# Layer 0, first strips: sums of squares and the shift's matrix product on four 32-column quarters of TensorE

## The chip, the cores and the metric

The kernel runs on one core of a Trainium2 chip. The metric is the time of one execution on the device, in microseconds (us). The engines that a core has are TensorE (PE; its weight loads are shown as PEld), VectorE (DVE), ScalarE (ACT), GpSimd (POOL) and SyncE (SP); SP, ACT and POOL also issue DMAs. Each engine works off its own instructions in the order in which they were written down, and waits on semaphores where another engine or a DMA has to come first.

## What is computed

A trunk of two layers on 1024 tokens of width 1024, all in float32. Layer 0 is a state-space mixer, layer 1 a forgetting attention. Only the head of layer 0 matters here:

```python
def _rms(x, g):
    xf = x.astype(jnp.float32)
    y = xf * lax.rsqrt(jnp.mean(xf * xf, axis=-1, keepdims=True) + EPS)
    return (y * g.astype(jnp.float32)).astype(x.dtype)

def _modulation(c, w, b, n):
    m = jax.nn.silu(c) @ w + b
    return jnp.split(m[:, None, :], n, axis=-1)
...
        if layer < N_A_LAYERS:
            shift, scale, gate = _modulation(c, a_mod_w[i], a_mod_b[i], 3)
            h = _rms(x, a_norm_g[i]) * (1.0 + scale) + shift
            y = _s5_mixer(h, a_w_in[i], ...)   # u, z = jnp.split(h @ w_in, 2, axis=-1)
```

So three vectors of 1024 come from silu(c) and a weight of 1024 x 3072; the first third of them is the shift.

## The kernel before, in words

x comes transposed: 8 strips of 128 features (partitions) by 1024 tokens, called xt. The normalisation is moved behind the projection. What is projected is x times the scale; the factor of each token, q2, is multiplied onto the result (`et`, line 323), and the shift's part, one number for each output row, is added as a bias. To get that number the activations have two more columns behind the 1024 tokens, columns 512 and 513 of the second half, that hold the shift (lines 300 to 303). Each float32 operand of a projection is split into a high and a low part (`aH`, `aL`, `w_hi`, `w_lo`), and three products of these are added up (`in_part`).

The modulation vectors are made by VectorE: `gemv` (line 132) multiplies a 128 x 1024 tile of the transposed weight with silu(c), spread over all partitions, and sums along the row. Tile n gives 128 entries of the vector.

The order of work, in the program's text:

1. A loop over 8 strips (line 272): load and gemv the tile of the scale (8 + k), load xt, make s_a, split the scaled strip into aH and aL, square it on ScalarE (`sqx`), and add up the squares over the partitions with two 128 x 512 float32 matmuls against a 128 x 128 matrix of 1/1024 (line 288). Each row of the result `msx` holds the same 1024 sums.
2. The projections `u01` for weight strips 0 and 1 over the 8 strips, tokens 0 to 767 (lines 290 to 292).
3. The load and split of weight strip 2, then 8 gemvs for the shift (lines 298 to 303), each followed by the two columns in aH (ScalarE) and aL (VectorE).
4. q2 from msx (`neg2_rsqrt`, line 153): six ScalarE and six VectorE operations on halves of 512.
5. Strip 2 in pieces of 512 and 256 tokens, then, for strips 0 to 3, the piece of 258 columns that holds the shift (c == 2 in `u_strip`), and strip 3's other pieces. For each strip `ut` (line 340, one buffer) is filled on ScalarE and written to memory (line 343).
6. The preparation of the state space: the angles `th`, `ang` (from line 373), sine and cosine (lines 387, 388), powers (`pwr`, `pwi`), and from the loads of B and C (`bb`, `bbs`, `x1m`, `x2m`, lines 469 to 473) the matrices `wm` and `moa`, which the matmuls `pin` and `pk` (lines 557, 569) read first. `pk` is a group of four matmuls that write 32 partitions each, on column quarters 0, 32, 64, 96 of TensorE.

The program's text is not the order in which the engines work: a scheduler writes down the order of each engine, by its own estimate of when things are ready, and `tc.issue_after` holds instructions behind a given one. All loads go through SP in the written order. The tiles of weights and x share seven buffers (tag `xw`), the projections' results two PSUM buffers (tag `pj`), so a copy out of PSUM must end before the second next piece starts.

Of the kernel before, what the change touches and what calls it, by code (L numbers as in the profile page):

```python
# [12 lines left out]
F32 = mybir.dt.float32  # L13
F32R = mybir.dt.float32r
BF16 = mybir.dt.bfloat16
AF = mybir.ActivationFunctionType
# [4 lines left out]
P = 128  # L21
D = 1024
KT = D // P
L = 1024
NG = 64
# [6 lines left out]
HL = L // 2  # L32
# [14 lines left out]
def trunk(tc, a, out):  # L47
    nc = tc.nc
    V, S, G, T, Q = nc.vector, nc.scalar, nc.gpsimd, nc.tensor, nc.sync
    top = ExitStack()  # L50
    with top:
# [4 lines left out]
        pj = top.enter_context(tc.tile_pool(name="pj", bufs=2, space=PSUM))  # L56
# [3 lines left out]
        def ctile(shape, nm, dt=F32):  # L60
            return cst.tile(shape, dt, name=nm, tag=nm)
# [4 lines left out]
        onesm = ctile([P, P], "onesm")  # L66
# [2 lines left out]
        G.memset(eps_t, EPS)  # L69
        one_t = ctile([P, 1], "one_t")  # L70
        G.memset(one_t, 1.0)
        vecs = ctile([P, 98], "vecs")
        c_b = modp.tile([P, D], F32, name="c_b", tag="c_b", bufs=1)
        Q.dma_start(out=c_b, in_=a["c"].broadcast_to([P, D]))
        Q.dma_start(out=vecs, in_=a["vecs"])
        vec, at0 = {}, 0
        for nm, w in (("a_g", 8), ("kv_g", 8), ("b_g", 8), ("b_glu", 8), ("kg", 1), ("qg", 1), ("modb", 64)):
            vec[nm] = vecs[:, at0:at0 + w]
            at0 += w
        fb_t = ctile([NH, 1], "fb_t")  # L80
# [48 lines left out]
        mod = ctile([P, 64], "mod")  # L129
# [5 lines left out]
        def modulate(n0, n1):  # L135
            for n in range(n0, n1):
                mw = mwp.tile([P, D], F32, name="modw", tag="modw")
                Q.dma_start(out=mw, in_=a["modw"][n])
                gemv(mw, n)

        def mod_bias(lo, hi, nm):
# [40 lines left out]
        with l0:  # L182
            s5 = l0.enter_context(tc.tile_pool(name="s5", bufs=1, reuse_waits="tile"))
# [66 lines left out]

            def mod_tile(n):
                mw = xp.tile([P, D], F32, name="mwx", tag="xw", bufs=7)
                d = Q.dma_start(out=mw, in_=a["modw"][n])
                gemv(mw, n)
                return d

            CH = ((0, 0, 512), (1, 0, 256), (1, 256, 514))
            TOK = (0, 512, 768)
# [9 lines left out]
            wu = pj.tile([P, HL], F32, name="wu", tag="pj")  # L268
            for _ in range(18):
                T.matmul(wu[:, 0:P], onesm, onesm, start=True, stop=True)  # L270
            mps = [pj.tile([P, HL], F32, name=f"msx{i}", tag="pj") for i in range(2)]
            for k in range(KT):
                mod_tile(8 + k)
                xt = xp.tile([P, L], F32, name="xt", tag="xw", bufs=7)
                Q.dma_start(out=xt, in_=a["xT"][:, k, :])
                if k < 2:
                    w01[k] = weight_strip(a["a_w_in"][k], [P, KT, P])
                V.scalar_tensor_tensor(out=s_a[:, k:k + 1], in0=mod[:, 8 + k:9 + k], scalar=sc1[:, k:k + 1], in1=ga[:, k:k + 1],
                                       op0=ALU.add, op1=ALU.mult)
                for i in range(2):  # L280
                    hi, xs = act[0][k][i][:, 0:HL], xt[:, HL * i:HL * i + HL]
                    S.activation(hi, xs, AF.Copy, scale=s_a[:, k:k + 1])
                    V.scalar_tensor_tensor(out=act[1][k][i][:, 0:HL], in0=xs, scalar=s_a[:, k:k + 1], in1=hi.bitcast(F32),
                                           op0=ALU.mult, op1=ALU.subtract)
                sq = xp.tile([P, L], F32, name="sqx", tag="sqx", bufs=2)
                sq_end = S.activation(sq, xt, AF.Square).ins
                for i in range(2):
                    T.matmul(mps[i], onesm, sq[:, HL * i:HL * i + HL], start=(k == 0), stop=(k == KT - 1))
            for k in range(KT):
                for e in range(2):  # L290
                    for c in range(2):
# [2 lines left out]
            Q.dma_start(out=raw2, in_=a["a_w_in"][2])  # L294
            w2 = [xp.tile([P, KT, P], F32R, name=f"w2{i}", tag=f"w2{i}") for i in range(2)]
            split(raw2, *w2)
            for k in range(KT):
                last_mod = mod_tile(k)
                hi, b = act[0][k][1][:, HL:], vec["modb"][:, k:k + 1]
                m = mod[:, k:k + 1].broadcast_to([P, 2])  # L300
                S.activation(hi, m, AF.Identity, bias=b)
                last_lo = V.scalar_tensor_tensor(out=act[1][k][1][:, HL:], in0=m, scalar=b, in1=hi.bitcast(F32),
                                                 op0=ALU.add, op1=ALU.subtract).ins
# [863 lines left out]
def pack(inp):  # L1167
    f = {k: np.asarray(v) for k, v in inp.items()}

    def strips(w, n=P):  # L1170
        m = w.shape[1]
        return w.reshape(KT, P, m // n, n).transpose(2, 1, 0, 3)

    def cols(v):
        return v.reshape(-1, P).T


    perm = np.arange(D).reshape(KT, 8, GC).transpose(0, 2, 1).reshape(-1)
# [6 lines left out]
    d = dict(  # L1185
        xT=f["x"][0].T.reshape(KT, P, L).transpose(1, 0, 2),
        c=f["c"].reshape(1, D),
        modw=modw.reshape(64, P, D),
        vecs=np.concatenate([cols(f["a_norm_g"][0]), cols(f["kv_norm_g"]), cols(f["b_norm_g"][0]), cols(f["a_b_glu"][0]),
                             np.concatenate([f["k_norm_g"]] * 2).reshape(P, 1),  # L1190
                             np.concatenate([f["q_norm_g"][0]] * 2).reshape(P, 1), cols(modb)], 1),
        f_bias=f["kv_f_bias"].reshape(NH, 1),
        A_re=f["a_A_re"][0].T, A_im=f["a_A_im"][0].T, log_dt=f["a_log_dt"][0].reshape(NG, 1),
        B_re=f["a_B_re"][0].transpose(1, 0, 2), B_im=f["a_B_im"][0].transpose(1, 0, 2),
        C_re=f["a_C_re"][0].transpose(2, 0, 1), C_im=f["a_C_im"][0].transpose(2, 0, 1),
        D=np.pad(f["a_D"].reshape(KT, 2, 4, GC).transpose(2, 3, 0, 1), ((0, 0), (0, 32 - GC), (0, 0), (0, 0))).reshape(P, 2 * KT),
        a_w_in=strips(f["a_w_in"][0]), a_w_glu=strips(f["a_w_glu"][0]), a_w_out=strips(f["a_w_out"][0]),
        kvq_w=np.concatenate([strips(f["kv_w"][:, D:2 * D], 256), strips(f["kv_w"][:, 0:D], 256),
                              strips(f["b_w_in"][0][:, 0:D], 256)], 0),
        kv_wf=strips(f["kv_w"][:, 2 * D:], NH)[0],  # L1200
        b_wz=strips(f["b_w_in"][0][:, D:]), b_w_out=strips(f["b_w_out"][0]),
    )
    return {k: np.ascontiguousarray(v) for k, v in d.items()}
# [13 lines left out]
```

## Time and profile before

| what | value |
|---|---|
| median of 3 runs | 1225.78 us (1220.67 to 1227.47) |
| the profiled execution | 1223.69 us |
| its span (first to last instruction) | 1221.9 us |
| mean granted TensorE clock | 0.987 of full speed |
| busy: TensorE, VectorE, ScalarE, GpSimd | 95%, 69%, 50%, 30% |
| busy from 0 to 160 us: TensorE, VectorE, ScalarE | 147.0, 136.7, 100.9 us |

Times in the profile count from the start of the span. In a list of instructions the columns are start, duration, engine, line, operation, output and inputs, shape and count, and in brackets the idle time of the engine ahead of it with what ended it. Rows that merge several instructions have a count, as x4. A float32 matmul shows as two records.

### The profile page before, as it was taken

To read this page: it belongs to the slowest core of one execution; us is meant where nothing else is said; L and a number is where in the kernel's file an instruction comes from. 1 tells how busy PE (TensorE), PEld (TensorE's weight loads), DVE (VectorE), ACT (ScalarE), POOL (GpSimd) and SP (SyncE) were. 2 spreads that over 40 slices of the span, in tenths; PEclk is the share of its full clock that TensorE was granted. 3 is DMA by queue.
4 is the path that set the end of the run, shared out by engine and by line. 5 is a ranking of instruction groups with operands and counts; after the bars stand their busy time and mean duration, and the time that the engine had idled before them with its cause. 6 is when DMAs were issued, how large, how long until landed. Compare 5 with 4: busy or idle time off the path is not lost.

```text
span 1221.9 us, 20599 instructions
## 1 busy us (share of the span) xinstructions
PE 1162.0 (95%) x7542; PEld 1017.3 (83%) x7542; DVE 848.9 (69%) x1724; ACT 605.1 (50%) x1138; POOL 367.8 (30%) x568
## 2 busy tenths in 40 slices
PE   8989898997899998899989999999999999999898
PEld 6778887887778876799989989998888888888686
DVE  7889899874498767746444664448787778887421
ACT  6565766665335324322213452227677777886310
POOL 4000000000000033600133463447576666764100
PEclk9999999998989999999999999999999999999999
DMA  9754666584974885247543277518796968871242
GB/s 352 220 173 117 171 169 164 154 233 126 334 249 129 281 312 167 90 154 233 200 148 139 83 214 152 156 70 182 132 188 124 171 122 155 156 138 27 94 165 78
DMA packets 113333, 205.30 MB, mean 168 GB/s; under 512 B 17072, under 2 KB 58160, under 8 KB 111696
## 3 DMA queue, kind: packets, MB, share of 16 engines
q1 hardware_dynamic: 86272, 161.44, 41.4%
q0 software_dynamic: 24960, 37.75, 18.1%
q10 hardware_dynamic: 2000, 4.79, 1.7%
q8 instruction: 60, 0.98, 0.3%
q14 instruction: 41, 0.34, 0.1%
HBM read 146.47 MB, written 46.20 MB: 158 GB/s over the span
## 4 chain that ended last, share of the span: by engine, by line
PE 57%; DVE 16%; DMA 12%; ACT 5%; issue 5%; SPq 2%; POOL 2%; ACTq 0%; POOLq 0%; DVEq 0%
PE tkps L851 16%; PE zb L112 7%; PE pj_f L112 5%; PE tp L1043 5%; DMA modw<-modw 4%; PE u L264 4%; PE ov L1049 3%; PE ov L1050 3%; PE sp L1010 3%; DMA v_d<-vt 3%; PE sp L1011 3%; PE pj_g L112 2%; DMA mwx<-modw 2%; PE f L112 2%; DVE w_lo L101 1%
## 5 line engine op out<-in xcount | busy, mean ns | idle before, releaser
L851 PE MATMUL tkps<-wvh,aH 128*128 128x256 f32 (+1 forms) x768 | 220.5, 287 | 7.3 <-DVE vt L863 4.0
L851 PE MATMUL tkps<-wvh,aL 128*128 128x256 f32 (+1 forms) x768 | 217.1, 283 | 1.4 <-DVE aL L167 1.4
L851 PE MATMUL tkps<-wvl,aH 128*128 128x256 f32 (+1 forms) x768 | 216.7, 282 | 0.0
L851 PEld LDWEIGHTS tkps<-wvh,aH 128*128 128x128 f32 x768 | 145.2, 189 | 9.8 <-DVE vt L863 4.9
L851 PEld LDWEIGHTS tkps<-wvh,aL 128*128 128x128 f32 x768 | 145.1, 189 | 2.1 <-DVE aL L167 1.8
L851 PEld LDWEIGHTS tkps<-wvl,aH 128*128 128x128 f32 x768 | 145.3, 189 | 0.3 <-issue 0.2
L1045 ACT ACTIVATE pth<-tp 128x512 fp32r<-128x512 f32 (+1 forms) x192 | 87.2, 489 | 61.4 <-PE ov L1049 34.7
L1018 ACT ACTIVATE pr<-pr,mx 128x128 f32<-128x128 f32 (+7 forms) x128 | 98.9, 773 | 22.4 <-DVE mx L1015 21.8
L1020 POOL TENSOR_SCALAR pr<-pr,sm 128x128 f32<-128x128 f32 (+7 forms) x128 | 96.2, 761 | 40.6 <-DVE sm L1019 40.5
L1046 DVE TENSOR_TENSOR ptl<-tp,pth 128x512 fp32r<-128x512 f32 (+1 forms) x192 | 101.3, 551 | 9.0 <-ACT pth L1045 8.6
L93 ACT ACTIVATE w_hi<-w_raw 128x1024 fp32r<-128x1024 f32 x49 | 51.6, 1053 | 86.4 <-PE pj_f L112 29.5
L1015 DVE CUSTOM_DVE_ANT_0 pr<-sp,fb 128x512 f32<-128x512 f32 (+3 forms) x128 | 72.8, 569 | 21.3 <-PE tp L1043 19.9
L1049 PE MATMUL ov<-pth,vhl 128*128 128x256 f32 x320 | 85.6, 299 | 0.1
L1043 PE MATMUL tp<-ident,pr 128*128 128x128 f32 x576 | 82.9, 273 | 0.0
L874 ACT ACTIVATE hsq<-tkps 128x256 f32<-128x256 f32 x64 | 24.6, 384 | 117.8 <-PE tkps L851 112.5
L132 DVE CUSTOM_DVE_ANT_0 modw<-modw,c_b 128x1024 f32<-128x1024 f32 x48 | 58.6, 1223 | 34.0 <-DMA modw<-modw 33.7
L1050 PE MATMUL ov<-ptl,vhl 128*128 128x256 f32 x320 | 81.0, 286 | 0.2 <-DVE ptl L1046 0.2
L1010 PE MATMUL sp<-kk,qs 128*128 128x256 f32 (+2 forms) x192 | 74.5, 388 | 2.2 <-DVE mx L1015 1.9
L1043 PEld LDWEIGHTS tp<-ident,pr 128*128 128x128 f32 x576 | 65.3, 140 | 7.1 <-POOL pr L1020 0.5
L794 POOL TENSOR_TENSOR sq<-sq,sq 128x512 f32<-128x512 f32 x12 | 19.0, 1585 | 173.3 <-ACT sq L790 173.3
L877 POOL TENSOR_TENSOR hms<-hms,nhalf 128x4 f32<-128x4 f32 x64 | 67.6, 1057 | 5.0
L876 POOL TENSOR_SCALAR hms<-hms 128x4 f32<-128x4 f32 x64 | 15.2, 237 | 176.3 <-DVE hms L875 172.4
(325 smaller groups left out, 3305.4 us busy)
## 6 DMA issues: line engine op xcount, KB each, us to landing
modw<-modw SPq DMA_DIRECT2D x48, 512.0 KB, 5.1
kk<-k_d POOLq DMA_DIRECT2D x32, 512.0 KB, 6.8
wvr<-kvq_w SPq DMA_DIRECT2D x12, 1024.0 KB, 5.5
mwx<-modw SPq DMA_DIRECT2D x16, 512.0 KB, 7.5
w_raw<-a_w_in SPq DMA_DIRECT2D x16, 512.0 KB, 5.2
v_d<-vt SPq DMA_DIRECT2D x32, 256.0 KB, 2.5
fb<-f_d SPq DMA_DIRECT2D x16, 512.0 KB, 8.9
vhl<-v_d POOLq DMA_DIRECT2D x16, 512.0 KB, 9.7
```

The source lines that it names most:

```text
L112: T.matmul(ps, w[wt][:, k, :], act[at][k][half], start=(k == k0 and n == 0), stop=(k == k1 and n == 2))
L851: T.matmul(ps[:, 0:nv], at, wt[:, k, 0:nv], start=(n == 0), stop=(n == 3 * KT - 1))
L877: G.tensor_tensor(out=ms, in0=ms, in1=nhalf, op=ALU.pow)
L1010: T.matmul(sp[:, 0:wm_], qsl, kk[:, 0, lo:lo + wm_], start=True, stop=False)
L1015: V.tensor_tensor_reduce(out=pr[:, lo:hi], in0=sp[:, 0:w_], in1=fb[:, lo:hi], scale=1.0, scalar=3e38 if m0 is None else m0, op0=ALU.add, o ...
L1018: S.activation(pr[:, 0:nk], pr[:, 0:nk], AF.Exp, scale=-1.0, bias=mx, accum_out=sm)
L1020: G.tensor_scalar(out=pr[:, 0:nk], in0=pr[:, 0:nk], scalar1=sm, scalar2=0.0, op0=ALU.mult, op1=ALU.add)
L1043: T.transpose(out=tp[:, b, :], in_=prs[qi][:, P * (b0 + b):P * (b0 + b) + P], identity=ident)
L1045: S.activation(pth[:, 0:m, dst], tp[:, 0:m, :], AF.Copy)
L1046: V.tensor_tensor(out=ptl[:, 0:m, dst], in0=tp[:, 0:m, :], in1=pth[:, 0:m, dst].bitcast(F32), op=ALU.subtract)
L1049: T.matmul(ov, vhl[:, b, :], pth[:, b - b0, :], start=(b == 0), stop=False)
L1050: end = T.matmul(ov, vhl[:, b, :], ptl[:, b - b0, :], start=False, stop=(b == nb - 1)).ins
```

## The change

Four things change, all in the head of layer 0.

- The sums of squares: the four squares of strips 0 to 3, and then those of 4 to 7, go as one group of four matmuls onto the four column quarters of TensorE, each 128 rows by 32 columns and 512 tokens, into 32 partitions of PSUM each (`quarters`). So 16 full matmuls become 4 groups of four. The result `msx` then holds four partial sums, 32 times each; ScalarE copies it to `mq`, and a matmul with a matrix of 1/32 (`o32`) for each half adds the four up over the partitions (`msy`).
- The shift: its weights come untransposed (`mod_sh`, 8 strips of 128 inputs by 1024 outputs), and the product is made by TensorE, with silu(c) as weights, 32 equal columns for each strip (`cs`): 4 groups of four matmuls (`psh`). ScalarE copies them to `shr`; eight small matmuls with two columns of `o32` (`pm`) add up the quarters and put the vector across the partitions. aH and aL of the two shift columns are then made out of PSUM (`pm`) instead of out of `mod`. The 8 gemvs and their 8 tile loads in the old layout go.
- Buffers: of the 8 strips of mod_sh, 0 to 3 use the `xw` buffers, 4 to 7 the buffers of `ut`, `bbs`, `x1m` and `x2m`. `sqx` has four buffers instead of two.
- The scratch memory for descriptors of DMAs that POOL issues is set to 8192.

```diff
+            def quarters(ps, ws, xs, first, last):
+                m = T.matmul(ps[96:P, :], ws[3], xs[3], start=first, stop=last).ins
+                with tc.issue_after(m):
+                    for q in range(3):
+                        T.matmul(ps[32 * q:32 * q + 32, :], ws[q], xs[q], start=first, stop=last)
...
-                sq = xp.tile([P, L], F32, name="sqx", tag="sqx", bufs=2)
+                sq = xp.tile([P, L], F32, name="sqx", tag="sqx", bufs=4)
                 sq_end = S.activation(sq, xt, AF.Square).ins
-                for i in range(2):
-                    T.matmul(mps[i], onesm, sq[:, HL * i:HL * i + HL], start=(k == 0), stop=(k == KT - 1))
+                sqs.append(sq)
+                if k % 4 == 3:
+                    for i in range(2):
+                        quarters(mps[i], [onesm[:, 0:32]] * 4, [t[:, HL * i:HL * i + HL] for t in sqs[-4:]], k == 3, k == KT - 1)
+            mq = xp.tile([P, L], F32, name="mq", tag="sqx", bufs=4)
+            for i in range(2):
+                S.activation(mq[:, HL * i:HL * i + HL], mps[i], AF.Copy)
+            mps = [pj.tile([P, HL], F32, name=f"msy{i}", tag="pj") for i in range(2)]
+            for i in range(2):
+                T.matmul(mps[i], o32, mq[:, HL * i:HL * i + HL], start=True, stop=True)
...
+            mws = []
             for k in range(KT):
-                last_mod = mod_tile(k)
+                pool, tag = ((s5, "ut"), (s5, "bbs"), (s5, "x1m"), (s5, "x2m"))[k - 4] if k >= 4 else (xp, "xw")
+                mws.append(pool.tile([P, D], F32, name="mws", tag=tag, bufs=7 if pool is xp else 1))
+                with tc.issue_after(last_x):
+                    last_mod = Q.dma_start(out=mws[k], in_=a["mod_sh"][k])
+            psh = [pj.tile([P, HL], F32, name=f"psh{i}", tag="pj") for i in range(2)]
+            for r in range(2):
+                for i in range(2):
+                    quarters(psh[i], [cs[:, k] for k in range(4 * r, 4 * r + 4)],
+                             [t[:, HL * i:HL * i + HL] for t in mws[4 * r:4 * r + 4]], r == 0, r == 1)
+            shr = xp.tile([P, D], F32, name="shr", tag="sqx", bufs=4)
+            for i in range(2):
+                S.activation(shr[:, HL * i:HL * i + HL], psh[i], AF.Copy)
+            pm = pj0.tile([P, NG], F32, name="pm", tag="dps")
+            for k in range(KT):
+                T.matmul(pm[:, 2 * k:2 * k + 2], shr[:, P * k:P * k + P], o32[:, 0:2], start=True, stop=True)
+            for k in range(KT):
                 hi, b = act[0][k][1][:, HL:], vec["modb"][:, k:k + 1]
-                m = mod[:, k:k + 1].broadcast_to([P, 2])
+                m = pm[:, 2 * k:2 * k + 2]
                 S.activation(hi, m, AF.Identity, bias=b)
                 last_lo = V.scalar_tensor_tensor(...)
...
-    nc = bacc.Bacc("TRN2", target_bir_lowering=False, num_devices=1)
+    nc = bacc.Bacc("TRN2", target_bir_lowering=False, num_devices=1, dynamic_dma_scratch_size=8192)
```

The scheduler writes a new order. The loads on SP behind the last strip of x, before:

```order
L275 DMA xt<-xT 128x1024
L294 DMA w_raw<-a_w_in 128x1024
L253 DMA mwx<-modw 128x1024 x8
L470 DMA bb<-B_re 64x1024
L471 DMA bb<-B_im 64x1024
L470 DMA bbs<-B_im 64x1024
L85 DMA w_raw<-a_w_in 128x1024
L471 DMA bbs<-B_re 64x1024
L470 DMA x1m<-C_re 64x1024
L471 DMA x1m<-C_im 64x1024
```

And after (mws are the strips of mod_sh; the first four are strips 4 to 7):

```order
L288 DMA xt<-xT 128x1024
L324 DMA mws<-mod_sh 128x1024 x4
L508 DMA bb<-B_re 64x1024
L315 DMA w_raw<-a_w_in 128x1024
L509 DMA bb<-B_im 64x1024
L324 DMA mws<-mod_sh 128x1024
L527 DMA fb_t<-f_bias 16x1
L324 DMA mws<-mod_sh 128x1024
L528 DMA dsk<-D 128x16
L324 DMA mws<-mod_sh 128x1024 x2
L85 DMA w_raw<-a_w_in 128x1024
L508 DMA x2m<-C_im 64x1024
```

The loads of B into bb stand ahead of the last strips now; those into x2m, bbs and x1m follow them, in this order, and wait for the matmuls psh that read these buffers.

ScalarE from the columns of the shift (aH out of mod) to the sine (the activation behind the table load, line 387), before:

```order
L301 ACTIVATE aH_1_165<-mod,vecs 128x2
L472 ACTIVATE x1m<-x1m,sg_pm 128x1024
L375 ACTIVATE th<-th 128x64 x7
L473 ACTIVATE x2m<-x2m 128x1024
L93 ACTIVATE w_hi<-w_raw 128x1024
L392 ACTIVATE ang_759<-th 128x448
L340 ACTIVATE ut<-et,bi 128x32x8
L340 ACTIVATE ut<-et,bi 128x64x8
L396 ACTIVATE ylo<-ang_759 128x64
L399 ACTIVATE xhi<-ang_759 128x64
L340 ACTIVATE ut<-et,bi 128x32x8
L387 ACT_TABLE_LOAD
```

After, from the last of the eight aH (out of pm; ahead of the eight stand now shr, x2m and x1m) to the same table load, line 425:

```order
L339 ACTIVATE aH_1_165<-pm,vecs 128x2
L413 ACTIVATE th<-th 128x64 x7
L93 ACTIVATE w_hi<-w_raw 128x1024
L378 ACTIVATE ut<-et,bi 128x32x8
L378 ACTIVATE ut<-et,bi 128x64x8
L378 ACTIVATE ut<-et,bi 128x32x8
L430 ACTIVATE ang_792<-th 128x448
L378 ACTIVATE ut<-et,bi 128x32x8
L378 ACTIVATE ut<-et,bi 128x64x8
L378 ACTIVATE ut<-et,bi 128x32x8
L425 ACT_TABLE_LOAD
```

x1m and x2m have moved ahead of the eight aH, and the three pieces of ut for strip 1 ahead of the sine. Each aH now also waits for the aL of the strip before it, since both engines read pm.

ScalarE in the second block of the state space, before (cT and sT are the tables of cosine and sine, r the gelu, which needs another table):

```order
L523 ACTIVATE cT<-sT 128x1024
L93 ACTIVATE w_hi<-w_raw 128x1024
L340 ACTIVATE ut<-et,bi 128x32x8
L631 ACT_TABLE_LOAD
L631 ACTIVATE r_1380<-py 128x512
L524 ACT_TABLE_LOAD
L524 ACTIVATE cT<-cT,hpi 128x1024
L525 ACTIVATE sT<-sT,tpi 128x1024
L543 ACTIVATE moa<-x1m 128x4x16
L631 ACT_TABLE_LOAD
```

And after:

```order
L561 ACTIVATE cT<-sT 128x1024
L549 DMA v_1330<-v_1329 64x1024 x2
L562 ACTIVATE cT<-cT,hpi 128x1024
L563 ACTIVATE sT<-sT,tpi 128x1024
L93 ACTIVATE w_hi<-w_raw 128x1024
L378 ACTIVATE ut<-et,bi 128x32x8
L669 ACT_TABLE_LOAD
L669 ACTIVATE r_1413<-py 128x512
```

cos and sin stand ahead of the gelu, and two of the three table loads are gone. Behind this place the order of every engine is that of before.

More of the change, by code (lines that the diff above doesn't have):

```diff
@@ L71, in trunk @@
         G.memset(one_t, 1.0)
-        vecs = ctile([P, 98], "vecs")
+        vecs = ctile([P, 106], "vecs")
         c_b = modp.tile([P, D], F32, name="c_b", tag="c_b", bufs=1)
@@ L76, in trunk @@
         vec, at0 = {}, 0
-        for nm, w in (("a_g", 8), ("kv_g", 8), ("b_g", 8), ("b_glu", 8), ("kg", 1), ("qg", 1), ("modb", 64)):
+        for nm, w in (("a_g", 8), ("kv_g", 8), ("b_g", 8), ("b_glu", 8), ("kg", 1), ("qg", 1), ("modb", 64), ("c", 8)):
             vec[nm] = vecs[:, at0:at0 + w]
@@ L137, in modulate @@
                 mw = mwp.tile([P, D], F32, name="modw", tag="modw")
-                Q.dma_start(out=mw, in_=a["modw"][n])
+                Q.dma_start(out=mw, in_=a["modw"][n - KT])
                 gemv(mw, n)
@@ L252, in mod_tile @@
                 mw = xp.tile([P, D], F32, name="mwx", tag="xw", bufs=7)
-                d = Q.dma_start(out=mw, in_=a["modw"][n])
+                Q.dma_start(out=mw, in_=a["modw"][n - KT])
                 gemv(mw, n)
-                return d
             CH = ((0, 0, 512), (1, 0, 256), (1, 256, 514))
@@ L274, in trunk @@
                 xt = xp.tile([P, L], F32, name="xt", tag="xw", bufs=7)
-                Q.dma_start(out=xt, in_=a["xT"][:, k, :])
+                last_x = Q.dma_start(out=xt, in_=a["xT"][:, k, :]).ins
                 if k < 2:
```

9 lines of the change are left out of this document (7 added, 2 removed).

## Prediction

> **What bounds the kernel now.** I read the page first. TensorE is busy for 95% of the span, but the share is an average, and the change lies in the first 60 us. So I took the windows there (columns: PE, PEld, DVE, ACT and POOL busy, granted clock, DMA share, GB/s).
>
> ```profile
> 10.00:15.00 5.00, 4.33 (x9) 2.33 (x10) 4.25 (x11) 3.85 (x5) 4.67 (x1) 0.66 1.02 406
> 38.00:40.00 2.00, 2.00 (x8) 1.25 (x7) 2.00 (x5) 0.06 (x1) 0.00 (x0) 1.00 1.01 381
> 42.00:44.00 2.00, 2.00 (x13) 1.73 (x13) 2.00 (x6) 2.00 (x6) 0.00 (x0) 1.00 1.02 231
> 60.00:70.00 10.00, 6.72 (x49) 6.38 (x50) 9.03 (x30) 8.13 (x16) 0.00 (x0) 0.97 0.42 111
> 90.00:100.00 10.00, 10.00 (x83) 9.23 (x81) 9.74 (x17) 7.07 (x14) 0.00 (x0) 1.00 0.33 97
> ```
>
> Up to 40 us the DMA is full at about 400 GB/s; behind that it stays full at half the rate, because then the loads of B and C run, which fill 64 partitions each. From 70 to 120 us TensorE has no gap, and VectorE is close behind it. Between the two lies a stretch where TensorE waits. The chain of waits names what it waited for (start, us, what):
>
> ```profile
> 26.62 7.70 DMA mwx<-modw
> 35.59 7.76 DMA mwx<-modw
> 43.38 10.86 DMA x1m<-C_im
> 54.31 1.15 ACT x1m L472
> 59.65 0.34 DVE et L323
> 60.13 6.23 PE u L264 x48
> ...
> 69.49 18.63 PE u L264 x96
> 88.12 0.44 PE pin L557 x4
> ```
>
> The shift's weights hold up the last load of C (x1m); that holds up ScalarE, ScalarE the angles (th, ang) on VectorE, these the copy that frees a PSUM buffer, and that TensorE. The timeline of TensorE has the gaps, and the start of each strip:
>
> ```profile
> 25.32 0.68 PE L264 MATMUL u<-aL,w_hi 128*128 128x256 f32 x1
> 43.69 0.40 PE L264 MATMUL u<-aH,w 128*128 128x512 f32 x1
> 52.10 0.28 PE L264 MATMUL u<-aH,w_hi 128*128 128x258 f32 x1
> 60.13 0.36 PE L264 MATMUL u<-aH,w 128*128 128x258 f32 x1 [2.10 <-DVE et L323]
> 69.49 0.76 PE L264 MATMUL u<-aH,w_hi 128*128 128x512 f32 x1 [3.15 <-DVE bi L337]
> 70.06 0.63 PE L264 MATMUL u<-aL,w_hi 128*128 128x512 f32 x1
> ```
>
> At 43.69 strip 2 starts, at 52.10 the columns that hold the shift. The gaps of 2.10 and 3.15 us cost 5.3 us; after the second the matmuls run at half clock (0.63 us where 0.40 is usual), six or so of them, some 1.4 us more.
>
> **The sums of squares.** Before, 16 float32 matmuls of 128x512 make them.
>
> ```profile
> 20.95 1.88 PE L288 MATMUL msx<-sqx,onesm 128*128 128x512 f32 x4
> 21.38 0.19 PEld L288 LDWEIGHTS msx<-sqx,onesm 128*128 128x128 f32 x1 [0.24 <-issue]
> 21.81 0.19 PEld L288 LDWEIGHTS msx<-sqx,onesm 128*128 128x128 f32 x1 [0.24 <-issue]
> 88.49 0.32 PE L569 MATMUL pk<-moa,bb 128*32 128x128 f32 x4
> 88.49 0.43 PE L569 MATMUL pk<-moa,bb 128*32 128x128 f32 x8
> 88.85 0.30 PEld L571 LDWEIGHTS pk<-dd,ident 128*128 128x128 f32 x2 [0.20 <-issue]
> ```
>
> One matmul is two records, 0.43 us apart, so 0.86 us; 16 are 13.8. What four on quarters cost, the kernel shows already: pk is such a group, four matmuls in eight records. A look at 88.53 to 88.56 holds four of them (first pk row), so four had begun within 0.07 us of each other. A record of 128 columns follows the one before after a quarter of 0.43, 0.11 us: in a row the eighth would start 0.75 us after the first. Yet all eight have ended 0.43 us after it began, so the four run side by side. I cost a group at two records (0.86) plus 0.1 for the switch of tiling (the 0.20 idle of the loads behind pk): 0.95 us. The sums take 4 groups, 3.8 us, and 2 full matmuls (msy), 1.7: 5.5 instead of 13.8. The other bound is four in a row, 3.44 us a group.
>
> The Trainium skill, "TensorE: Matmul & The Clock Gate", section "Measured speedup vs the span model", gives 2.38 times for three column tiles; at that share of the ideal, a group would be an estimated 1.1 us, and the sum 1 us longer.
>
> TensorE then has, from 25.3 on, what it had until 43.69 without its last three pairs of sums (18.4 - 3 x 1.72 = 13.2 us), one pair of groups (1.9) and msy (1.7): it is free at 42.1. With fewer matmuls its clock may stay low for longer (0.66 in the window 10 to 15, after an idle stretch): 0 to 3.4 us; I take 1.5, so 43.6.
>
> **The shift.** Eight gemvs leave VectorE:
>
> ```profile
> L132 DVE CUSTOM_DVE_ANT_0 mwx<-mwx,c_b x16: 1159/1215/1225, 8.4 to 48.4; 128x1024 f32<-128x1024 f32 x16
> 49.63 0.30 ACT L301 ACTIVATE aH<-mod,vecs 128x2 fp32r<-128x2 f32 x1 [2.19 <-DVE mod L132]
> 50.98 0.21 DVE L302 SCALAR_TENSOR_TENSOR aL<-mod,vecs,aH 128x2 fp32r<-128x2 f32 x1
> 54.31 1.15 ACT L472 ACTIVATE x1m<-x1m,sg_pm 128x1024 f32<-128x1024 f32 x1 [4.38 <-DMA x1m<-C_im]
> 55.36 1.12 ACT L375 ACTIVATE th<-th 128x64 f32<-128x64 f32 x7
> ```
>
> 8 x 1.22 = 9.7 us, but most of that time VectorE then idles. The same 4 MB of weights must land. Before, the seventh strip landed at 43.35 (35.59 + 7.76); now six of the eight loads of B and C are behind all of them, so I take 43.3 (42 to 45). TensorE is ready then. psh: 4 groups, 3.8 us, to 47.4. Four pm matmuls (two loads each like the 0.30 of pk's last) 1.2, then strip 2's two pieces (52.10 - 43.69 = 8.4) with four pm between them (1.2): the columns of the shift are reached at 58.2, 6.1 later than before.
>
> The weights of strips 4 to 7 lie in the buffers of ut, bbs, x1m, x2m, so six loads now wait for psh: issued from 47.2, 1.57 MB. At the 231 GB/s of the window they need 6.8 us; with some 2 us to start they land at 56 (at 400 GB/s: 53). SyncE has further behind them only the writes of ut and the strips of weights, which aren't due before 60. On ScalarE the eight aH now stand behind x2m and x1m, so they start at 57.2 instead of 37 to 50, and each waits for the aL before it: 8 x (0.30 + 0.21) = 4.1, bounds 2.5 to 5. The angles are behind them: th ends at 62.5 instead of 56.5, 6 us late. Shift columns and angles are therefore both late by 6. What TensorE gains is that its two gaps shrink, since VectorE's copies for strips 0 and 1 are no longer behind the wait for th: its strip 3 starts at about 72 (when strip 1's ut, below, frees a buffer of et), against 69.49 and the 1.4 of slow clock, so 1 us behind.
>
> The sine is what is late next:
>
> ```profile
> 57.44 2.14 DVE L383 SCALAR_TENSOR_TENSOR th<-ang,th 128x512 f32<-128x512 f32 x3
> 60.16 1.77 ACT L340 ACTIVATE ut<-et,bi 128x256 f32<-128x256 f32 x2
> 64.04 0.26 ACT L387 ACTIVATE ang<-th 128x64 f32<-128x64 f32 x1
> u_d<-ut SPq DMA_DIRECT2D x8, 512.0 KB, 3.5
> 85.22 0.62 DVE L197 TENSOR_TENSOR wm<-wm,tm 128x448 f32<-128x448 f32 x1
> ```
>
> Before, it came at 64.04, ahead of strip 1's ut. Now it stands behind it, and ut has one buffer. The copies of strip 0 followed the end of th (56.5) by 3.2 us; two of the three steps of 0.7 between are now behind them, so they start 1.8 after 62.5, at 64.3. The ut of strip 0, three pieces of about 2.3 us in all (1.77 for two), ends at 67, its write lands 3.5 us later, ut of strip 1 takes 2.3 and the table 1.3 (rows below): the sine comes at 74.2, 10 us late. From the sine to wm VectorE needed 21.2 us (85.22 + 0.62 - 64.04 = 21.8, less the sine); the same work without its idle pieces is 19 to 20, so wm is ready at 94 instead of 85.8. TensorE reached pin at 88.1 and would now come at about 89: it waits 5 us, and pin stands 6 us later than before. A gap of that length costs half clock behind it as the one of 3.15 did: 7.4.
>
> **What is given back.**
>
> ```profile
> 124.83 1.28 ACT L631 ACT_TABLE_LOAD   x1
> 126.74 1.28 ACT L524 ACT_TABLE_LOAD   x1
> 129.22 1.22 DVE L197 TENSOR_TENSOR r<-cT,v 128x1016 f32<-128x1016 f32 x1 [2.18 <-ACT cT L524]
> 116.20 0.69 DVE L323 TENSOR_TENSOR et<-u,q2x 128x512 f32<-128x512 f32 x1 [0.64 <-PE u L264]
> ```
>
> ScalarE's order now has cos and sin of this block ahead of the gelu, so two table loads (2.56 us) go; VectorE's wait of 2.18 for cT goes with them. With its idle 0.64 and small ones before it, VectorE gives back about 3. Behind this the order is the old one, and the chain runs on to the end: 7.4 - 3 = 4.4 us longer.
>
> **Edits at nothing.** cs, o32 and 4 KB more of vecs lie in the first 10 us under DMA. mq and shr (four copies of 0.7 us) lie beside matmuls of the first strips and the last psh group. The halved scratch touches POOL's loads alone:
>
> ```profile
> L970 POOL DMA_DIRECT2D kk<-k_d x32 | 20.2, 633 | 27.0 <-PE sp L1011 24.7 <-PE sp L1013 2.3
> ```
>
> Their issue waits 27 us for TensorE anyway; that slack covers it. Without it, doubling the issue (20.2 us) would be its price.
>
> **The sum.** The profiled execution took 1223.69 us, span 1221.9; it lies 2.1 under the median of 1225.78. 1223.7 + 4.4 = 1228.1. A measurement of this kernel tells about 0.5% (6.1 us) from no change.
>
> **The rivals.**
> Half clock kept (slower): without the 13.8 us of sums TensorE's work for the first strips is bursts of about 1 us in a strip of 2.8 us. If the clock stays at one half until about 32, psh starts 3.4 later and all behind it: 1231.5. For it speaks the 0.66 of the window; against it, that strips at half speed nearly fill the time. It decides if psh starts after 46. [...]
> Nothing given back (slower): VectorE is full (9.74 of 10) and stays late by 8 through the scan: 1232.
> Early loads (faster): the six loads meet an empty queue, and land at 400 GB/s by 53; the angles are then only 3 us late, pin doesn't wait, strip 3 starts 2 us earlier than before with its clock kept, and the tables' 2.6 come on top: 1219, down to 1216. Against it: in the window 42 to 44, where these loads run, a full DMA moved 231.
> Quarters one after another: sums 10 us and psh 10 us longer, 1248. pk's rows speak against it.
> POOL's loads stall in layer 1 with half the scratch: half of a doubled issue (20.2) would be 10 us, 1238; nothing in the trace shows how full it is.
>
> **How the numbers follow.** Forecast 0.48; early loads 0.16, of which half passes 6.1 us (0.08); nothing given back 0.18; half clock 0.10; in a row 0.05; POOL 0.03. Faster by over 0.5%: 0.08. Within: 0.48 + 0.08 = 0.56. Slower: 0.18 + 0.10 + 0.05 + 0.03 = 0.36. The range: 1218 takes in most of the early loads, 1236 the unknown 3.4 us of clock and 1 us a bound of the aH on top of "nothing given back"; left out are the serial quarters, POOL and the far ends, under 0.2.
>
> **What would show it.** Right: psh groups of about 0.95 us from 43 to 45; x1m landing at 55 to 57; aH and aL taking turns from 57 on; the sine at 72 to 76; TensorE waiting 3 us or more for wm at pin; two table loads fewer before the second scan. Wrong: psh groups over 1.5 us; x1m before 53.5 or after 59; no wait at pin; any difference that arises behind 300 us.

## The result, and the profile after

The changed kernel takes 1236.43 us (median of 4 runs, 1235.56 to 1238.72) against 1225.07 for the kernel before (4 runs beside them): 1.0099 times as long, with a 95% interval of 1.0074 to 1.0124. The profiled execution has a span of 1233.9 us against 1221.9, so 12 us more. The forecast was 1228.1 and the range ended at 1236.0: the direction of the likeliest case was right, the size less than half of what came.

TensorE's busy time is the same to the tenth (1162.0 us of both spans), so all the 12 us more are idle time of TensorE (matmuls at low clock count as busy). The windows of the first stages show where. Columns as before, behind the window and its length: PE, PEld, DVE, ACT and POOL busy, granted clock, DMA share, GB/s.

```profile
35.00:40.00 5.00, 5.00 (x33) 2.69 (x32) 1.41 (x2) 1.99 (x4) 0.00 (x0) 1.00 1.03 228
45.00:50.00 5.00, 2.98 (x16) 0.92 (x20) 2.98 (x5) 0.17 (x1) 0.00 (x0) 0.66 0.43 154
98.00:102.00 4.00, 0.00 (x0) 0.00 (x0) 0.00 (x0) 2.80 (x6) 0.11 (x1) 0.50 0.86 212
106.00:110.00 4.00, 4.00 (x20) 4.00 (x21) 3.90 (x6) 0.00 (x0) 0.00 (x0) 0.50 0.02 4
```

From 35 to 40 us, while the shift's strips are still due, the DMA is full (1.03) and yet moves 228 GB/s. TensorE is busy for 2.98 us between 45 and 50, at 0.66 of its clock, not at all from 98 to 102, and works at half clock until behind 110. Before, it had no gap from 70 to 120. The chain of waits (start, us, what) names the links:

```profile
26.50 11.78 DMA bb<-B_re
38.34 8.54 DMA mws<-mod_sh
53.29 1.24 SPq L508
55.86 5.70 DMA x1m<-C_im
...
73.02 2.98 DMA u_d<-ut
...
94.92 7.32 DMA bbs<-bb
106.35 5.24 PE u L263 x24
```

A load of bb, 11.78 us long, holds up the last strip of mod_sh, which lands at 46.88; that holds up psh, psh the load of x1m, which lands at 61.56 (before: 54.24). The write of ut and the swap of bbs were not links of before's chain. The last row is the same piece of work that took 2.95 us there: half clock. TensorE's timeline has the two large gaps:

```profile
40.87 1.02 PE L309 MATMUL msy<-mq,o 128*128 128x512 f32 x2
47.02 1.03 PE L280 MATMUL psh<-mws,cs 128*32 128x512 f32 x1 [5.13 <-DMA mws<-mod_sh]
51.48 0.60 PE L283 MATMUL psh<-mws,cs 128*32 128x512 f32 x3
52.93 0.47 PE L263 MATMUL u<-aH,w 128*128 128x512 f32 x1
64.51 0.36 PE L263 MATMUL u<-aH,w_hi 128*128 128x258 f32 x1 [2.03 <-DVE aL L340]
103.79 1.09 PE L595 MATMUL pin<-ident,wm 128*128 128x128 f32 x4 [8.93 <-DVE wm L197]
```

TensorE is free at 41.9, waits 5.13 for the strip, starts psh at half clock and ends it at 52.1; strip 2 starts at 52.93 (43.69 before); at pin it waits 8.93 for wm, and pin stands at 103.8 (88.0 in the same list of before; its chain of waits has 88.1). On ScalarE, between the two:

```profile
61.66 1.15 ACT L510 ACTIVATE x1m<-x1m,sg_pm 128x1024 f32<-128x1024 f32 x1 [3.15 <-DMA x1m<-C_im]
62.72 0.24 ACT L339 ACTIVATE aH<-pm,vecs 128x2 fp32r<-128x2 f32 x1
63.25 0.26 ACT L339 ACTIVATE aH<-pm,vecs 128x2 fp32r<-128x2 f32 x1 [0.29 <-DVE aL L340]
...
67.40 1.13 ACT L413 ACTIVATE th<-th 128x64 f32<-128x64 f32 x7 [0.42 <-DVE th L197]
...
76.09 2.21 ACT L378 ACTIVATE ut<-et,bi 128x256 f32<-128x256 f32 x3 [0.58 <-DMA u_d<-ut]
78.31 1.28 ACT L425 ACT_TABLE_LOAD   x1
79.61 0.26 ACT L425 ACTIVATE ang<-th 128x64 f32<-128x64 f32 x1
```

The aH and aL take turns, a round each 0.55 us; the sine stands behind strip 1's ut, which waits for the write of strip 0's. All that is as the prediction had it, only later: from the landing of x1m to the sine each of its terms is within 0.5 us. One wait is new: VectorE's, for the swapped bbs, ahead of wm. The next rows are VectorE's, then the DMA issues around the swap, of after and of before (there the last of its four pieces), and then the four pieces of after and of before (KB of one, median us from issue to landing).

```profile
102.36 0.62 DVE L197 TENSOR_TENSOR tm<-bbs,rvi 128x448 f32<-128x448 f32 x1 [4.66 <-DMA bbs<-bb]
103.02 0.62 DVE L197 TENSOR_TENSOR wm<-wm,tm 128x448 f32<-128x448 f32 x1
```

```profile
92.40 1.45 SPq L624 DMA_DIRECT2D uu<-u_d  x2
94.39 2.46 ACTq L522 DMA_DIRECT2D bbs<-bb  x4
```

```profile
79.55 0.47 ACTq L484 DMA_DIRECT2D bbs<-bb  x1
82.45 1.48 SPq L586 DMA_DIRECT2D uu<-u_d  x2
```

```profile
bbs<-bb ACTq DMA_DIRECT2D x4, 128.0 KB, 7.2
```

```profile
bbs<-bb ACTq DMA_DIRECT2D x4, 128.0 KB, 2.9
```

Before, the four pieces of the swap were under way ahead of the two loads of uu, which wait only for the u strips. Now the strips are 10 us late and the angles 15.6, so the order is turned round: the swap is issued 2 us behind the loads of uu, 512 KB each, on a full DMA (its share is 1.02 from 94 to 98), and a piece takes 7.2 us to land instead of 2.9.

What follows pin: the first scan is 19.5 us later than before (125.10 against 105.61), the second 18.4 (151.61 against 133.19), the first matmul of pj_g 18.9 (318.1 against 299.2). The first of pj_o is 13.5 later (408.5 against 395.0), the end 12.

### The profile page after: what moved, and what is told of

The parts are those of the page before. It is cut to its first block, busy times and chain, and to the rows that moved or that the text cites. A ratio compares the mean times of both kernels' runs of the same rounds, so it can differ in the third digit from the quotient of the medians.

```text
span 1233.9 us, 20697 instructions
## 1 busy us (share of the span) xinstructions
PE 1162.0 (94%) x7594; PEld 1015.9 (82%) x7594; DVE 838.7 (68%) x1708; ACT 606.0 (49%) x1141; POOL 368.5 (30%) x569
## 4 chain that ended last, share of the span: by engine, by line
PE 56%; DVE 17%; DMA 15%; ACT 4%; issue 4%; SPq 2%; POOL 2%; ACTq 0%; POOLq 0%; DVEq 0%
PE tkps L889 17%; PE zb L112 6%; PE pj_f L112 5%; DMA modw<-modw 5%; PE tp L1081 4%; PE ov L1088 3%; PE u L263 3%; PE ov L1087 3%; PE sp L1048 3%; PE z L263 2%; PE sp L1049 2%; DMA v_d<-vt 2%; PE pj_g L112 2%; PE f L112 2%; DVE modw L132 1%
## 5 line engine op out<-in xcount | busy, mean ns | idle before, releaser
L889 PEld LDWEIGHTS tkps<-wvh,aL 128*128 128x128 f32 x768 | 145.0, 189 | 0.3 <-issue 0.2
L1056 ACT ACTIVATE pr<-pr,mx 128x128 f32<-128x128 f32 (+7 forms) x128 | 98.9, 773 | 23.0 <-DVE mx L1053 22.5
L1058 POOL TENSOR_SCALAR pr<-pr,sm 128x128 f32<-128x128 f32 (+7 forms) x128 | 96.1, 759 | 41.9 <-DVE sm L1057 41.8
```

The source lines that it names most:

```text
L889: T.matmul(ps[:, 0:nv], at, wt[:, k, 0:nv], start=(n == 0), stop=(n == 3 * KT - 1))
L1056: S.activation(pr[:, 0:nk], pr[:, 0:nk], AF.Exp, scale=-1.0, bias=mx, accum_out=sm)
L1058: G.tensor_scalar(out=pr[:, 0:nk], in0=pr[:, 0:nk], scalar1=sm, scalar2=0.0, op0=ALU.mult, op1=ALU.add)
```

## The experiments

All starts in the table come from each run's own profiled execution, in us; the ratio is to the kernel before on the same chip, with its 95% interval. "Wait" is TensorE's longest wait for wm at a pin. Single starts vary: before and e_scratch, which engines work off in the same order, differ by 1.2 us at x1m and pin, and by 3.2 at the first matmul of pj_g.

| kernel | ratio | x1m scaled | sine | wait | pin | second scan |
|---|---|---|---|---|---|---|
| before | 1 | 54.3 | 64.0 | 0.7 | 88.0 | 133.2 |
| changed | 1.0099 [1.0074, 1.0124] | 61.7 | 79.6 | 8.9 | 103.8 | 151.6 |
| e_sums | 1.0016 [0.9994, 1.0038] | 52.7 | 57.0 | 0.7 | 84.5 | 130.0 |
| e_shift | 1.0081 [1.0051, 1.0112] | 59.8 | 78.2 | 8.5 | 101.9 | 148.8 |
| e_scratch | 1.0004 [0.9982, 1.0025] | 53.1 | 62.9 | 0.7 | 86.8 | 132.0 |
| e_bb_last | 1.0075 [1.0048, 1.0102] | 55.9 | 73.8 | 8.8 | 97.9 | 145.0 |
| e_bufs | 1.0078 [1.0049, 1.0108] | 57.0 | 75.3 | 8.3 | 98.9 | 148.8 |
| e_gate2 | 1.0140 [1.0101, 1.0179] | 62.4 | 56.3 | 0.7 | 100.4 | 147.0 |
| e_bufs_gate2 | 1.0057 [1.0035, 1.0080] | 52.4 | 55.5 | 0.7 | 93.5 | 139.8 |
| e_cis | 1.0137 [1.0110, 1.0163] | 61.8 | 79.7 | 8.6 | 103.6 | 153.0 |
| e_warm | 1.0125 [1.0103, 1.0148] | 60.1 | 78.5 | 8.4 | 102.1 | 150.9 |
| e_pm | 1.0082 [1.0051, 1.0113] | 61.4 | 73.8 | 1.3 | 97.0 | 142.4 |
| e_bufs_pm | 1.0001 [0.9981, 1.0020] | 54.0 | 66.9 | 0.7 | 89.4 | 134.8 |
| e_bufs_gate2_pm | 1.0015 [0.9997, 1.0032] | 55.8 | 58.7 | 0.7 | 91.7 | 137.8 |

### The parts, each alone

**e_sums**: before, with the quarters for the sums of squares (the first half of the diff), the smaller scratch, and the gemvs kept.

> Before, with only the sums of squares on quarters; the shift stays eight gemvs on VectorE. The cost-is-in-the-shift theory: TensorE comes to strip 2 some 8 us earlier but then waits for C's last load (54.3 as before) as it did, so pin stays within 2 us of 88.1 and the time is 1219 to 1227 (before: 1225). The rival that the sums are to blame (their clock, or mq and msy on ScalarE and TensorE): 1229 or more. A further rival, that the shorter sums pay as they stand: pin at 86 or earlier, under 1219.

The time is that of before: the sums cost nothing, and they give nothing. Pin came at 84.5, which is where the further rival had it and not within 2 us of 88.1, but the time under 1219 that it went with did not come (median 1224.24). The windows show what became of the shorter sums; of before, then of e_sums:

```profile
0.00:25.00 25.00, 20.75 (x79) 13.84 (x80) 16.86 (x43) 15.11 (x19) 14.22 (x25) 0.93 0.91 340
```

```profile
0.00:25.00 25.00, 18.30 (x79) 13.35 (x80) 16.43 (x43) 14.62 (x18) 14.37 (x26) 0.80 0.93 343
```

TensorE has less to do and is given less to do it with: it idles 2.45 us more and the clock falls from 0.93 to 0.80, while the loads come at the same pace (340 and 343 GB/s, the DMA at 0.91 and 0.93). That they set the pace is argued from this, not tried. Of some 8 us less work, strip 2 starts 2.0 earlier (41.65 against 43.69; e_scratch, whose program has before's order, started it at 42.81).

**e_shift**: the changed kernel with the old sums.

> The changed kernel with the sums of squares made as before (16 full matmuls); only the shift on TensorE's quarters. The cost-is-in-the-shift theory: the last strip of mod_sh lands at about 47 as in the changed kernel; TensorE is busy with the sums until about then and doesn't go to half clock, so psh ends within 1.5 us of 52 and x1m lands at 60 to 62, pin at 102 to 104: 1234 to 1237. The rival that the quarters of the sums cost the time: about 1226.

The ratio is as expected, x1m and pin lie within 0.2 us of the early ends of their ranges: the shift alone is the loss. TensorE is busy until 45 here, and psh runs at full clock, from 46.8 to 50.4.

**e_scratch**: before with half the DMA scratch.

```diff
-    nc = bacc.Bacc("TRN2", target_bir_lowering=False, num_devices=1)
+    nc = bacc.Bacc("TRN2", target_bir_lowering=False, num_devices=1, dynamic_dma_scratch_size=8192)
```

> The kernel before with 8192 instead of 16384 bytes for the DMA scratch, nothing else. The shift theory: no change, 1223 to 1227, no new wait on GpSimd's loads. The rival that the smaller scratch stalls GpSimd's loads in layer 1: up to 1235, with time of kk's loads above 20.2 us.

No change, and the issue of kk's loads takes what it took:

```profile
L970 POOL DMA_DIRECT2D kk<-k_d x32 | 20.2, 632 | 27.1 <-PE sp L1011 24.7 <-PE sp L1013 2.3
```

### The late strips

**e_bb_last**: the mark behind which the loads of B and C may go is the eighth strip's issue in the changed kernel, but two loads of bb slipped in between the strips; setting the mark at the fourth strip makes the order come out with all eight strips ahead.

```diff
-                    last_mod = Q.dma_start(out=mws[k], in_=a["mod_sh"][k])
+                    d = Q.dma_start(out=mws[k], in_=a["mod_sh"][k])
+                    if k == 3:
+                        last_mod = d
```

> The changed kernel with the two loads of bb behind all eight strips of mod_sh instead of behind four. The late-strip theory: no 64-partition load is in the queue while the strips come, so the last strip lands at 42 to 43 instead of 46.9, psh ends at about 46.5 without half clock (52.1), x1m lands at 55 to 57 (61.6), sine and pin move by the same 5 to 6 us: 1229 to 1232. The rival that the angles' place on ScalarE behind x2m, x1m and the eight aH costs it, whenever the strips land: 1235 or more.

The strips did what was expected. The window and TensorE of this run:

```profile
35.00:40.00 5.00, 5.00 (x33) 2.86 (x32) 1.42 (x2) 2.22 (x4) 0.00 (x0) 1.00 1.05 398
```

```profile
43.00 0.59 PE L280 MATMUL psh<-mws,cs 128*32 128x512 f32 x1 [0.86 <-ACT q2x L155]
97.88 1.09 PE L597 MATMUL pin<-ident,wm 128*128 128x128 f32 x4 [8.85 <-DVE wm L197]
```

Without a 64-partition load among them the strips come at 398 GB/s instead of 228, psh no longer waits for one, and x1m, sine and pin each come 5.7 to 5.9 us earlier. But the time falls by less than expected: 1.0075 against 1.0099, with intervals that overlap. This run is of use in another way: here psh starts at 43.0, x1m is there at 55.9 and the sine at 73.8, which is the prediction's own schedule (43.3, 56, 74.2). Even on it pin comes at 97.9, not at 94, and the time is 9 us over before, not 4.4.

**e_bufs**: strips 4 to 7 in buffers that x and the squares have left, so that no load of B or C waits for psh.

```diff
-                pool, tag = ((s5, "ut"), (s5, "bbs"), (s5, "x1m"), (s5, "x2m"))[k - 4] if k >= 4 else (xp, "xw")
-                mws.append(pool.tile([P, D], F32, name="mws", tag=tag, bufs=7 if pool is xp else 1))
+                tag, n = ("xw", 7) if k < 7 else ("sqx", 4)
+                mws.append(xp.tile([P, D], F32, name="mws", tag=tag, bufs=n))
```

> The changed kernel with strips 4 to 7 of mod_sh in the buffers of x (three) and of the squares (one) instead of those of ut, bbs, x1m and x2m: no load of B or C waits for psh. The theory that the lateness comes down the chain strips, psh, six loads, x1m: the last strip lands at 42 to 43, x1m at 51 to 53, th ends at 58 to 60, the sine at 68 to 71, pin at 92 to 95 (103.8), and the time is 3 to 6 us over before (the changed kernel: 12). The rival that the order on ScalarE and VectorE costs it (aH and aL taking turns, the sine behind a second ut, cis behind the ut of later strips), whatever the loads do: pin at 97 or later, 8 us or more over before.

From the chain of waits of this run:

```profile
38.95 5.39 DMA mws<-mod_sh
44.36 12.54 DMA x1m<-C_im
```

The first theory was too hopeful. The strips wait for x's buffers, the last lands at 44.3, and the last load of C, which no longer waits for psh, takes 12.54 us in a queue of its own kind: x1m came 4.7 us earlier but not by 51 to 53, and pin at 98.9 fits the rival. Late loads are one cause; there is a second behind them.

### What is behind the loads

**e_gate2**: one line of the order. q2_end is the last instruction of the scale of x on VectorE.

```diff
-            gate.enter_context(tc.issue_after(last_lo))
+            gate.enter_context(tc.issue_after(q2_end))
```

> The changed kernel with one rule of the order changed: the angles (th, ang, sine, powers) no longer stand behind the shift's last aL but behind the scale of x (q2x), so that VectorE and ScalarE make them in the 15 us in which they wait for psh. x1m lands as late as in the changed kernel (60 to 62). The theory that the lateness reaches pin through the angles alone: sine at 48 to 52 instead of 79.6, pin at 86 to 92 without a wait over 3 us, time within 4 us of before. The rival that the late shift columns and the late x1m themselves hold TensorE up (strips 0 and 1 can't be finished, ut has one buffer): pin at 95 or later, 6 us or more over before.

The sine comes at 56.3 (48 to 52 expected), TensorE no longer waits at pin, and yet pin stands at 100.4: the rival held. The angles are not the only late path; TensorE's own strips are the other, with the late shift columns. (Its runs spread from 1232.5 to 1245.6 and the profiled one is the shortest, so the trace doesn't show all of its 1.0140.)

**e_bufs_gate2**: both edits.

> Both edits, the strips' other buffers and the angles behind q2x. If both chains are what the change costs, nothing of it is left and TensorE's shorter sums begin to pay: x1m at 51 to 53, pin at 82 to 86 (before: 88), time 0 to 6 us under before. The rival that something else of the change costs time: over before by 3 us or more.

The rival held again: still 1.0057, and pin at 93.5. TensorE's gaps and the window around them:

```profile
57.70 0.36 PE L263 MATMUL u<-aH,w_hi 128*128 128x258 f32 x1 [1.52 <-DVE nr L490]
59.91 0.58 PE L263 MATMUL u<-aL,w_hi 128*128 128x258 f32 x1 [0.77 <-DVE aL L340]
```

```profile
60.00:65.00 5.00, 4.90 (x21) 4.60 (x22) 4.92 (x20) 2.36 (x10) 0.00 (x0) 0.50 0.00 0
```

The shift columns reach TensorE one by one, because each aH waits for the aL before it, and these have other work of VectorE between them. Behind gaps that leave TensorE busy for 2.67 of 5 us (55 to 60) the clock is at 0.50 for a whole stretch.

**e_cis**: a try at the new wait for bbs.

```diff
-            S.activation(cis, ci, AF.Copy, scale=sg_mp)
+            V.tensor_scalar(out=cis, in0=ci, scalar1=sg_mp, scalar2=None, op0=ALU.mult)
```

> The changed kernel with cis, a scaling of ci by a sign, made by VectorE where ci is ready instead of by ScalarE, where it stands behind the ut of two later strips. The theory that this place in ScalarE's order is the 4.7 us wait for bbs that the prediction left out: bbs's swap is issued some 3 us earlier, the wait falls to 1 to 2, pin comes 3 to 4 us earlier (100 to 101), and the time falls by 2 to 4 against the changed kernel. The rival that the swap's landing (7 us on a busy queue) sets it: pin within 1 us of 103.8.

A miss. The first piece of the swap was issued at 93.5 instead of 94.4, not 3 us earlier and still behind the loads of uu (92.4); VectorE waited 4.9 instead of 4.7, and pin stayed at 103.6. So the place of cis was not the cause of that wait. What speaks for the loads of uu is a comparison over all the kernels of the table, not an edit of its own. In the six that issue the swap behind them (changed, e_shift, e_bb_last, e_bufs, e_cis, e_warm) the median of its four pieces takes 6.5 to 7.6 us to land, and VectorE waits 4.0 to 4.9 for it. In the eight that issue it ahead the median is 2.2 to 3.3, and VectorE doesn't wait for it.

**e_warm**: five more full matmuls on TensorE ahead of psh, whose results nothing reads.

```diff
+            for _ in range(5):
+                T.matmul(psh[0], onesm, sqs[-1][:, 0:HL], start=True, stop=True)
```

> The changed kernel with five more full 128x512 matmuls on TensorE between msy and psh (their result is overwritten by psh), which fill its wait for the last strip. The half-clock theory: psh's records come 0.43 us apart instead of 0.85 at the start, psh ends at 50.3 to 50.8 instead of 52.1, and x1m, sine and pin each come 1.3 to 1.7 us earlier: 1 to 2 us less than the changed kernel. The rival that the clock is no part of it: psh ends within 0.5 us of 52.1.

The clock was the cause of psh's slow start: with TensorE busy, its records come 0.43 us apart from the first, and psh ends at 50.5 instead of 52.1.

```profile
41.29 4.56 PE L327 MATMUL psh<-sqx,onesm 128*128 128x512 f32 x10
46.92 0.62 PE L280 MATMUL psh<-mws,cs 128*32 128x512 f32 x1 [1.07 <-DMA mws<-mod_sh]
47.37 0.59 PE L280 MATMUL psh<-mws,cs 128*32 128x512 f32 x1
49.95 0.61 PE L283 MATMUL psh<-mws,cs 128*32 128x512 f32 x3
```

x1m, sine and pin came 1.2 to 1.7 earlier, nearly as expected. No gain in the time can be shown (1.0125 and 1.0099, overlapping).

**e_pm**: the eight pairs of columns copied out of PSUM once.

```diff
+            pmv = xp.tile([P, 2 * KT], F32, name="pmv")
+            V.tensor_copy(out=pmv, in_=pm[:, 0:2 * KT])
...
-                m = pm[:, 2 * k:2 * k + 2]
+                m = pmv[:, 2 * k:2 * k + 2]
```

> The changed kernel with pm copied to SBUF by one VectorE instruction, and the aH and aL made from the copy: ScalarE no longer waits for each aL before the next aH. If the taking of turns (0.55 us a step from 62.7 to 67.2) costs what the prediction gave it (4.1 less the 8 x 0.21 or so that remains), the eight aH end by 65, th ends 2 us earlier than 68.5, pin 2 us earlier than 103.8, and the time is 1 to 3 us less than that of the changed kernel. The rival that the other waits in between take it up again (the write of ut, the swap of bb): pin within 1 us of 103.8.

ScalarE of this run, and the DMA issues around the swap:

```profile
62.41 1.58 ACT L341 ACTIVATE aH<-pmv,vecs 128x2 fp32r<-128x2 f32 x8
64.85 1.14 ACT L415 ACTIVATE th<-th 128x64 f32<-128x64 f32 x7 [0.86 <-DVE th L197]
...
72.46 1.28 ACT L427 ACT_TABLE_LOAD   x1
73.76 0.26 ACT L427 ACTIVATE ang<-th 128x64 f32<-128x64 f32 x1
75.45 2.25 ACT L380 ACTIVATE ut<-et,bi 128x256 f32<-128x256 f32 x3 [0.67 <-DMA u_d<-ut]
```

```profile
88.11 1.15 ACTq L524 DMA_DIRECT2D bbs<-bb  x2
90.97 1.95 SPq L626 DMA_DIRECT2D uu<-u_d  x2
```

More than expected. The eight aH take 1.6 us together instead of 4.3, and th comes 2.55 earlier; with that the planner puts the sine ahead of strip 1's ut again, as it stood before the change, so the sine comes 5.9 earlier, the swap is issued ahead of the loads of uu, and pin comes 6.8 earlier. TensorE's wait at pin is gone (1.3 at most). The time, 1.0082, is not clear of the changed kernel's.

**e_bufs_pm**: the edits of e_bufs and e_pm.

> Strips in other buffers and pm copied; the angles still behind the shift. In the run with other buffers alone x1m came at 57.0 and pin at 98.9. If the two delays add up: aH done 3 us earlier, the sine stands ahead of the second ut now and comes 6 us or more earlier than 75.3, pin at 90 to 94, time 3 to 6 us over before. The rival that ut's one buffer and VectorE's order give pin whatever comes before: pin at 96 or later, 8 us or more over before.

Better than expected: 1.0001, pin at 89.4, no wait there.

**e_bufs_gate2_pm**: all three.

> All three edits: strips in other buffers, the angles behind q2x, pm copied. Without the copy, pin came at 93.5, TensorE having spent 57.7 to 66 on shift columns that came one by one, at half clock. If that was the last cost: the shift columns run through at full clock, pin at 86 to 90, time within 3 us of before. If it is faster than before by more than the measurement's 0.5%, the shorter sums pay. The rival that the change holds something more: 6 us or more over before.

1.0015, within 3 us as expected of the first theory, but not by its way: pin came at 91.7, not at 86 to 90, and the shift columns still met a low clock (0.66 from 60 to 65). The earlier angles add nothing once the other two are mended. No version beats before.

## Why the prediction was wrong

The chain from the strips to pin was right, two of its sizes were too small, and one wait was left out; most of the points come out of the traces of after, e_bb_last and e_bufs_pm.

**Right.** A group on quarters costs two records: 0.86 us apart from start to start at full clock (0.95 predicted), so nothing runs in a row. (The Trainium skill, "TensorE: Matmul & The Clock Gate", section "Measured speedup vs the span model", would have made it an estimated 1.1 us: the trace is faster.) TensorE was free at 41.9 (42.1, with clock 43.6). The sign that was named for the half-clock rival, psh behind 46, came all the same (47.0), but from the strip. GpSimd's scratch costs nothing (e_scratch). The sums gain nothing by themselves (e_sums). x1m is what the angles wait for, psh what x1m waits for: 9.5 us from the end of psh to the landing of x1m (52.1 to 61.6), 8.6 predicted (47.4 to 56). From the landing of x1m to the sine 18.05 us (61.56 to 79.61), 18.2 predicted.

**The step that failed first** is "The same 4 MB of weights must land. Before, the seventh strip landed at 43.35 (35.59 + 7.76); now six of the eight loads of B and C are behind all of them, so I take 43.3 (42 to 45)". Six are behind, but the two that stayed ahead were enough: with them in the queue the full DMA moved 228 GB/s instead of 398 in the same 5 us (after against e_bb_last), a load of bb took 11.78 us, and the last strip landed at 46.88. The half clock at psh's start, priced at the other end of the chain and not here, added 1.6 (e_warm). Together psh ended at 52.1 instead of 47.4, which e_bb_last gives back: 5.9 us at pin. The number that was needed stood in a row that the prediction itself quoted (231 GB/s from 42 to 44), and it was used for the six loads but not for the two.

**The second** is "the same work without its idle pieces is 19 to 20, so wm is ready at 94". From the sine to the start of wm's last step VectorE took 23.4 us (79.61 to 103.02), and the same 23.3 in e_bb_last: 4.65 of it is the wait for the swap, a term that the prediction does not have; without it the 19 to 20 would have held. The prediction moved the sine by 10 us and the u strips by much less, and did not ask which transfers change places by that. That is the 3.9 us by which pin in e_bb_last (97.9) is later than predicted (94). That the loads of uu slow the swap rests on the comparison above; no edit turned that order alone.

**The third** is "VectorE gives back about 3". At most 1.1 us of that is seen, from the first scan to the second (26.5 us instead of 27.6; e_scratch, in the order of before, took 26.8). The wait of 2.18 for cT went as predicted, but VectorE now waits 2.12 for py, a result of TensorE, in the same stretch. From pin to the first scan more was lost: 21.3 us, against 17.6 before. Of these 3.7 us 2.1 are no new loss: before, wm stood ready 2.1 us ahead of pin (85.8 and 88.0), so VectorE is later by that already at wm. The rest fits the half clock behind the 8.9 us wait. It lasts until behind 110, the same 24 matmuls take 5.24 us instead of 2.95, where the prediction had taken 1.4 from a gap of 3.15, and VectorE waits 2.40 for v, which comes from TensorE's next results (0.39 before). In e_bufs_pm, without the wait, pin to scan is 18.1.

**A difference behind 300**, which the prediction named as a sign against it, is there, as a gain of 5.4 us: from the first pj_g to the first pj_o 90.4 us instead of 95.8. It is not the lateness that is given back: e_bufs_pm, which is hardly late, needs 91.5 for it, the other kernels with the shift on TensorE need 90.5 to 93.4, and the three with the gemvs 94.5 to 95.8. What the shift on TensorE spares this stage was not tried. No term of the prediction has this gain: at the second scan the kernel is 18.4 us late where the forecast had 4.4, and that it ends only 12 late, nearer to the forecast, is luck.

So at pin, 9.8 us more than predicted: 5.9 from the late strips, 3.9 from the swap. And what both rest on: the loss has two causes, the late loads and the turns of aH and aL, that hide each other. Mending the loads alone (e_bufs) takes 4.9 us off pin, the copy of pm alone 6.8, both 14.4 of 15.8; in the time the first two show no gain that can be told from none, both together all of it. The prediction counted the turns (4.1 us, measured 4.3), but as a small term of the sum. The runs show them as one of two causes of the whole loss: without them (e_pm) the sine stands ahead of ut and the swap ahead of uu again.

## What to carry to other kernels

When work moves to a quiet engine, follow the buffers and queues that it takes: here the engine time was as predicted, and the loss came from weights in other tensors' buffers, from two small loads in a full queue, and from two engines that take turns on one small tile. Price every transfer in a queue at the rate of its own shape, and ask at each moved step which two transfers or instructions now change places. When undoing one suspect changes little, undo two together before dropping either.

## What the runs showed of the hardware

A full queue with loads of 64 partitions among those of 128 moved 228 GB/s, and 398 without them, over the same 5 us with the DMA at 1.03 and 1.05. Four float32 matmuls on 32-column quarters run fully side by side: a round of four is 0.86 us from start to start, what one full matmul of the same 512 columns takes. TensorE was at half clock behind a wait of 5.1 us for the first of psh's records; behind the wait of 8.9 it was still at 0.50 in the window 106 to 110. The Trainium skill, "TensorE: Matmul & The Clock Gate", section "HAM oscillation — how this bites in real kernels", says that gaps of TensorE above some 3.4 us are to be avoided, since the next burst then starts at the low clock. These two waits agree, but shorter ones did it here too. In e_bufs_gate2_pm, behind a wait of 1.86 us, records of 258 columns came 0.21 us apart instead of 0.12 from 61.4 to 64.6; in e_shift, behind 1.68 us, psh ran at full clock. And in e_bufs_gate2, behind 55 to 60 with 2.67 of 5 us busy and no wait above 1.52, TensorE was busy for 4.90 of the next 5 us at 0.50.
